# Block 2's first feed-forward with its last eight inner tiles split into latent and context, and queries ahead of keys

## The chip, the cores and the metric

The kernel is one program on one core of a Trainium2 chip. The metric is the time of one execution on the device, in microseconds (us); lower is better. Five engines work side by side, each through its own queue in order: TensorE (PE in the profile; PEld is its loading of weights), VectorE (DVE), ScalarE (ACT), GpSimd (POOL) and SyncE (SP), which here only issues transfers.

## The reference, cut to what matters

Two transformer blocks follow each other. The second has 512 latent tokens `x` and 256 context tokens `ctx`, all 1024 wide. What the change touches is the second block's first feed-forward and the projections behind it:

```
def _modnorm(x, g_pre, shift, scale):   return _rmsnorm(x, g_pre) * (1 + scale) + shift
def _residual(x, y, g_post, gate, w):   return x + w * gate * _rmsnorm(y, g_post)
def _swiglu(h, w1, w3, w2):             return (silu(h @ w1) * (h @ w3)) @ w2       # inner width 2816

x     = _residual(x,     _swiglu(_modnorm(x,     g[0], m[0],  m[1]),  w1, w3, w2), g[1], m[2],  0.5)
h_ctx = _residual(h_ctx, _swiglu(_modnorm(h_ctx, g[0], mc[0], mc[1]), w1, w3, w2), g[1], mc[2], 0.5)
# then, for latent and context tokens, from _modnorm(., g[2], m[3], m[4]) @ w_in:
#   cq (768 wide)  -> rmsnorm -> @ w_uq  -> queries of 8 heads (64 without, 32 with rotation)
#   ckv (256 wide) -> rmsnorm -> @ w_ukv -> keys and values of 8 heads;  kr (32 wide) -> rotated key part
#   qa, ka, va     -> neighbourhood attention
```

Queries are needed for the latent tokens alone, keys and values for all 768 tokens.

## The kernel before

All activations stand with features on the 128 partitions and tokens along the free axis, so a product is `weights (stationary) x tokens (moving)`. Every operand is split into a high and a low part (`whi`, `wlo` for weights; `XH`, `XL` for the latent tokens, `CH`, `CL` for the context, `hh`, `hl` for the inner layer), and each product is three matmuls: high x high, high x low, low x high.

**Weights.** `Emitter` holds a list of units. A unit is one 128x1024 block of weights (`raw`, 512 KB, three buffers), loaded by SP. It is split into two chunks of 512 columns: ACT copies the high part (`whi`, line 132), then DVE or POOL subtracts it (`wlo`, line 136; `low_parts(V, G)` says that chunks alternate between DVE and POOL, `low_parts(V, V)` that DVE makes all). Four chunk buffers run round, so the split can be at most four chunks ahead of PE. A unit over one segment of tokens is 24 matmuls (8 steps of the inner dimension x 3), recorded at line 231, into the PSUM tiles `psg` and `pss` in turn, four in all.

**Work between matmuls.** A generator handed to `background(gen, pace)` is advanced by one slot each time the matmuls put into the program add up to `pace` nanoseconds; `drain` runs it to its end. So a generator's instructions stand in each engine's queue between those of the matmuls' own helpers. A scheduler then orders each engine's queue; engines never reorder at run time.

**The feed-forward** (`ffn`, line 1123) has 22 inner tiles in groups of 6, 8 and 8. For each tile `pair` multiplies by a unit of `w1` and a unit of `w3`; the evacuations `e1`, `e3` (lines 1132 to 1141, and `hh`, `hl`) form the inner layer. Then `products` multiplies a group by eight units of `w2` and adds into `y` (line 1174). `XC` is the mode with two segments, 258 columns of context (two of them shift columns) and 512 of latent tokens; `XO` has two segments of latent tokens alone, 258 and 256 columns.

**The residual** (`update`, line 1178) works on a range of tokens of `y`: sums of squares and their reciprocal root (small DVE steps named `rsm`, a small matmul for the sums, line 330, and one that spreads the result, line 349), then for each of 8 feature tiles: `y` times the factor (line 1231, six of eight on POOL), `x` plus scaled `y` (line 1228, DVE), the new high part and the square (ACT), the low part (line 1212, DVE), the sum of squares (line 1214, seven of eight on POOL). At its end it asks for the next norm's factor `R4`, which every later evacuation multiplies by.

**The end of the feed-forward before**: the last group's eight tiles run over all 768 tokens; `products` runs over columns 256 to 767, then over 0 to 255 with `update(256, 768)` in the background; then `kv(XC_A)` (two units for `ckv`, one for `kr`, over the context and the upper latent half) with `update(0, 256)` in the background; `drain`; `kv(X_B)` (the same three units for the lower latent half, loaded again); six units of `cq`; four of `wuk` (keys), one of `wuv` (values, six chunks of tokens, spilled to memory as `v_d` through `vst`); two and four of `wuq` (queries, spilled as `qr_d`, `qn_d`). Neighbourhood attention (`open_na`) follows.

Of the kernel before, what the change touches and what calls it, by code (L numbers as in the profile page):

```python
# [6 lines left out]
F32 = mybir.dt.float32  # L7
F32R = mybir.dt.float32r
# [250 lines left out]
def emit(tc, d, out, dbg=None, stop=None):  # L259
# [756 lines left out]
                V.tensor_scalar_mul(cf(o), cf(o), w)  # L1016
        yield

    def shift_cols(kx, kc):
        todo = [(S["XH"], S["XL"], 512 + i, mod(kx)) for i in range(2)]  # L1020
        if kc is not None:
            todo += [(S["CH"], S["CL"], 0, mod(kx)), (S["CH"], S["CL"], 1, mod(kc, 1))]
        for h_, l_, o, m_ in todo:
            act(h_[:, :, o], m_)
            sub_lo(V, l_[:, :, o], m_, h_[:, :, o])
# [97 lines left out]
    def ffn(tag, w1, w3, w2, mode, ntok, pool, Rk, down, head, tail):  # L1123
# [26 lines left out]
        for gi, (k0, nk) in enumerate(grp):  # L1150
            em.call(newh)

            def pair(j, m, a=0, k0=k0):
                proj(w1[k0 + j], 128, m, e1(j), (tag, 1, a))
                proj(w3[k0 + j], 128, m, e3(j), (tag, 3, a))

            def products(segs, gi=gi, k0=k0, nk=nk):
                for n in range(8):
                    em.gemm(w2[n][:, k0:k0 + nk, :], 128, lambda si: st["h"], segs,
                            lambda si, ps, n=n: down(gi, n, segs[si][0], segs[si][1], ps), kt=nk)  # L1160

            for j in range(head(pair) if gi == 0 else 0, nk):
                pair(j, mode)
            if gi == 2:
                tail(products)
            else:
                products([(512, 256), (0, 512)] if ntok == 768 else [(0, 512)])

# [9 lines left out]
    def update(c0, c1, p, b, a, bc=None, ac=None, spilled=False, late=1500):  # L1178


        xe = min(c1, 512)
        n = xe - c0
        Ry, acc = S["Ry"][:, c0:c1], S["accy"][:, c0:c1]
        ctx = c1 > 512
        CR, SQ = {}, {}
# [5 lines left out]

        def parts(k):

            yield S["y"][:, k, c0:xe], S["x"][:, k, c0:xe], b, a, S["XH"][:, k, c0:xe], S["XL"][:, k, c0:xe], 0
            if ctx:
                yield S["y"][:, k, xe:c1], CR[k], bc, ac, S["CH"][:, k, 2:258], S["CL"][:, k, 2:258], n

        load(0)
        load(1)
# [55 lines left out]
    def no_head(pair):  # L1255
        return 0

    def f1_tail(products):
        products([(256, 512)])
        em.low_parts(V, V)  # L1260
        em.call(lambda: shift_cols(3, 3))
        em.background(lambda: update(256, 768, S["fpa"], B1X, A2X, B1C, A2C, True), 1150)
        products([(0, 256)])
        em.drain()

    em.call(open_f1)
# [5 lines left out]
    def open_pj():  # L1272
        dp = S["dram"]
        S["qn_d"] = dp.tile([4, 128, 2, 512], F32R, name="qn_d")
        S["qr_d"] = dp.tile([2, 128, 2, 512], F32R, name="qr_d")
        S["kn_d"] = dp.tile([4, 128, 2, 768], F32R, name="kn_d")
        S["kr_d"] = dp.tile([32, 2, 768], F32R, name="kr_d")
        S["v_d"] = dp.tile([8, 128, 6, 128], F32R, name="v_d")
        for n_ in ("yp", "fpa", "mp"):
            pools.close(n_)  # L1280
        p = S["pj"] = pools.open("pj", side="right")
        S["QH"] = p.tile([128, 6, 512], F32R, name="QH")
        S["QL"] = p.tile([128, 6, 512], F32R, name="QL")
        S["Rq"] = p.tile([128, 512], F32, name="Rq")
        S["aq"] = p.tile([128, 512], F32, name="aq")
        S["tmpq"] = p.tile([128, 512], F32, name="tmpq")
        for n_, w in (("rotT", 128), ("ropeC", 512), ("ropeS", 512)):
            S[n_] = p.tile([128, w], F32, name=n_)
            SP.dma_start(S[n_], d[n_])

    def open_kvp():
# [7 lines left out]
        S["tmpk"] = p.tile([128, 768], F32, name="tmpk")  # L1299
        S["krt"] = p.tile([32, 768], F32, name="krt")  # L1300
        S["krs"] = p.tile([32, 2, 768], F32R, name="krs")

    def lat_evac(j, hi, lo, acc, g, nt, last, done):
        def f(t0, n, ps, b):
# [90 lines left out]
        proj(d["wkr"], 32, mode, kr_evac, "kr")  # L1395

    em.call(open_kvp)
    em.depth(DEEP, 2)
    em.background(lambda: update(0, 256, S["fpa"], B1X, A2X, spilled=True), 1200)
    kv(XC_A)  # L1400
    em.depth(DEEP, 2)
    em.drain()
    em.call(lambda: dumps((("x2", lambda: S["x"]),)))
    em.call(open_pj)
    em.low_parts(V, G)
    kv(X_B)
    em.depth(DEEP)
    for j in range(6):
        proj(d["wq"][12 + j], 128, XO, lat_evac(j, "QH", "QL", "aq", "gq", 512, j == 5, rq_done), "cq")
    for j in range(4):  # L1410
        em.gemm(d["wuk"][j], 128, lambda si: (S["KH"], S["KL"]), [(512, 256), (0, 512)],
                nope_evac(j, "kn_d", "Rkv", 768), kt=2)
    em.gemm_tok(d["wuv"], 512, lambda si: (S["KH"], S["KL"]), [(128 * c, 128) for c in range(6)], v_evac, kt=2)
    for j in range(2):
        em.gemm(d["wuq"][4 + j], 128, lambda si: (S["QH"], S["QL"]), FULL, qr_evac(j), kt=6)
    for j in range(4):
        em.gemm(d["wuq"][j], 128, lambda si: (S["QH"], S["QL"]), FULL, nope_evac(j, "qn_d", "Rq", 512), kt=6)


    NA = {}  # L1420
# [1 line left out]
    def open_na():  # L1422
        em.flush_after()
        pools.close("pj")
        pools.close("kvp")
        p = S["onap"] = pools.open("onap", side="right")
        S["ONH"] = p.tile([128, 4, 512], F32R, name="ONH")
# [422 lines left out]
            SP.dma_start(out[:, k, c0:c1], x)  # L1850
            yield

    def f2_tail(products):
        products([(256, 256)])
        em.low_parts(V, V)
        em.background(lambda: finish(256, 512), 1100)
        products([(0, 256)])
        em.background(lambda: finish(0, 256), 1000)
        em.drain()
# [120 lines left out]
```

## Time and profile before

| what | value |
| --- | --- |
| median of 3 runs | 2838.61 us (2836.48 to 2839.34) |
| profiled execution | 2835.9 us; its trace spans 2834.1 us |
| mean granted TensorE clock | 0.984 of full speed |
| busy share of the span | PE 97%, PEld 85%, DVE 57%, ACT 39%, POOL 31% |
| weights and data moved | 316.95 MB, mean 112 GB/s |

The time between the trace's span and the profiled execution (1.8 us) lies around the program. Matmuls are pipelined and their ends are modelled: a busy PE may still be issuing slower than it could, so the distance between the starts of matmuls says more than the busy time.

### The profile page before, as it was taken

To read this page: it belongs to the slowest core of one execution; us is meant where nothing else is said; L and a number is where in the kernel's file an instruction comes from. 1 tells how busy PE (TensorE), PEld (TensorE's weight loads), DVE (VectorE), ACT (ScalarE), POOL (GpSimd) and SP (SyncE) were. 2 spreads that over 40 slices of the span, in tenths; PEclk is the share of its full clock that TensorE was granted. 3 is DMA by queue.
4 is the path that set the end of the run, shared out by engine and by line. 5 is a ranking of instruction groups with operands and counts; after the bars stand their busy time and mean duration, and the time that the engine had idled before them with its cause. 6 is when DMAs were issued, how large, how long until landed. Compare 5 with 4: busy or idle time off the path is not lost.

```text
span 2834.1 us, 42927 instructions
## 1 busy us (share of the span) xinstructions
PE 2737.6 (97%) x16308; PEld 2405.3 (85%) x16308; DVE 1619.8 (57%) x3308; ACT 1091.7 (39%) x2198; POOL 870.4 (31%) x723
## 2 busy tenths in 40 slices
PE   9999999999999889899999999979999999899997
PEld 7889988898878667788888888878889998899897
DVE  6554422377756999555223233496676876834346
ACT  4323322355534222243222122354455665633233
POOL 2213323443324233342111111442333224323224
PEclk9999999999999999999999999989999999999998
DMA  3212222443235658332121221334643425432224
GB/s 130 79 62 96 91 96 97 132 120 108 81 105 183 202 194 290 118 108 68 52 75 60 60 68 60 91 118 155 177 104 102 133 62 161 133 97 90 92 95 127
DMA packets 115998, 316.95 MB, mean 112 GB/s; under 512 B 21680, under 2 KB 35376, under 8 KB 115536
## 3 DMA queue, kind: packets, MB, share of 16 engines
q1 hardware_dynamic: 115792, 314.21, 35.8%
q8 instruction: 129, 2.11, 0.3%
q14 instruction: 77, 0.63, 0.1%
HBM read 279.09 MB, written 13.83 MB: 103 GB/s over the span
## 4 chain that ended last, share of the span: by engine, by line
PE 81%; DVE 13%; issue 3%; ACT 2%; DMA 1%; POOL 0%; SPq 0%; POOLq 0%; DVEq 0%; ACTq 0%
PE psg L231 49%; PE pss L231 23%; DVE wlo L136 2%; DVE wa L999 2%; DVE wx L999 1%; PE pss L277 1%; PE pst L831 1%; PE pss L278 1%; PE pss L279 1%; PE pst L1735 1%; PE pst L1721 1%; PE pss L1532 1%; PE pst L828 0%; DVE XL L1212 0%; DVE mg L1228 0%
## 5 line engine op out<-in xcount | busy, mean ns | idle before, releaser
L136 POOL TENSOR_TENSOR wlo<-raw,whi 128x512 fp32r<-128x512 f32 (+1 forms) x450 | 592.7, 1317 | 1571.3 <-ACT whi L132 1518.1
L132 ACT ACTIVATE whi<-raw 128x512 fp32r<-128x512 f32 (+1 forms) x844 | 522.7, 622 | 928.0 <-PE psg L231 593.1
L136 DVE TENSOR_TENSOR wlo<-raw,whi 128x512 fp32r<-128x512 f32 x394 | 306.5, 778 | 454.0 <-ACT whi L132 453.2
L231 PE MATMUL psg<-xh,wlo 128*128 128x264 f32 (+2 forms) x1104 | 361.0, 327 | 1.9 <-DVE wlo L136 1.9
L231 PE MATMUL psg<-xl,whi 128*128 128x264 f32 (+2 forms) x1104 | 362.1, 328 | 0.8 <-DVE xl L403 0.7
L231 PE MATMUL psg<-xh,whi 128*128 128x264 f32 (+2 forms) x1104 | 360.7, 327 | 0.1
L231 PE MATMUL psg<-XH,whi 128*128 128x256 f32 (+3 forms) x984 | 307.7, 313 | 2.4 <-DVE krt L1341 1.4
L231 PE MATMUL psg<-XH,wlo 128*128 128x256 f32 (+3 forms) x984 | 307.6, 313 | 0.0
L231 PE MATMUL psg<-XL,whi 128*128 128x256 f32 (+3 forms) x984 | 307.3, 312 | 0.0
L231 PEld LDWEIGHTS psg<-xh,wlo 128*128 128x128 f32 x1104 | 208.5, 189 | 18.7 <-DVE wlo L136 2.1
L231 PEld LDWEIGHTS psg<-xl,whi 128*128 128x128 f32 x1104 | 208.5, 189 | 18.6 <-DVE xl L403 1.5
L231 PEld LDWEIGHTS psg<-xh,whi 128*128 128x128 f32 x1104 | 208.6, 189 | 17.1 <-ACT whi L132 0.4
L231 PE MATMUL pss<-XL,whi 128*128 128x256 f32 (+2 forms) x600 | 190.8, 319 | 5.9 <-DVE XL L1212 5.9
L231 PEld LDWEIGHTS psg<-XH,whi 128*128 128x128 f32 (+1 forms) x984 | 185.0, 188 | 12.1 <-issue 3.1
L231 PEld LDWEIGHTS psg<-XH,wlo 128*128 128x128 f32 (+1 forms) x984 | 185.2, 188 | 10.5 <-issue 0.2
L231 PEld LDWEIGHTS psg<-XL,whi 128*128 128x128 f32 (+1 forms) x984 | 185.3, 188 | 9.3
L231 PE MATMUL pss<-XH,wlo 128*128 128x256 f32 (+2 forms) x600 | 191.1, 319 | 1.2 <-DVE wlo L136 1.2
L231 PE MATMUL pss<-XH,whi 128*128 128x256 f32 (+2 forms) x600 | 190.5, 318 | 0.5 <-DVE fs L1132 0.5
L231 PEld LDWEIGHTS pss<-XL,whi 128*128 128x128 f32 x600 | 114.3, 191 | 14.2 <-DVE XL L1212 7.2
L231 PEld LDWEIGHTS pss<-XH,wlo 128*128 128x128 f32 x600 | 114.9, 192 | 10.1 <-DVE wlo L136 1.6
L231 PEld LDWEIGHTS pss<-XH,whi 128*128 128x128 f32 x600 | 114.4, 191 | 7.5 <-DVE fs L1132 0.7
L999 DVE CUSTOM_DVE_ANT_0 wa<-wa,sb 128x1024 f32<-128x1024 f32 x72 | 106.6, 1483 | 4.4 <-DMA wa<-wa 3.9
(562 smaller groups left out, 6461.7 us busy)
## 6 DMA issues: line engine op xcount, KB each, us to landing
raw<-w SPq DMA_DIRECT2D x142, 512.0 KB, 3.4
raw<-wi SPq DMA_DIRECT2D x96, 512.0 KB, 3.3
wa<-wa SPq DMA_DIRECT2D x72, 512.0 KB, 4.2
raw<-wq SPq DMA_DIRECT2D x38, 512.0 KB, 3.5
raw<-wu SPq DMA_DIRECT2D x32, 512.0 KB, 4.1
raw<-wd SPq DMA_DIRECT2D x32, 512.0 KB, 4.2
raw<-wb SPq DMA_DIRECT2D x24, 512.0 KB, 3.3
raw<-wo SPq DMA_DIRECT2D x24, 512.0 KB, 3.6
```

What stands on the lines that cost most here:

```text
L132: s.nc.scalar.activation(h, raw, AF.Copy)
L136: eng.tensor_sub(l, raw, h.bitcast(F32))
L231: nc.tensor.matmul(out, l, r, start=(k == 0 and m == 0), stop=(k == it.kt - 1 and m == 2))
L277: T.matmul(o, wh, xh, start=first, stop=False)
L278: T.matmul(o, wh, xl, start=False, stop=False)
L279: T.matmul(o, wl, xh, start=False, stop=last)
L831: T.matmul(o, x[:, c, :], vs[:, c, :], start=False, stop=c == b and m == 1)
L999: V.tensor_tensor_reduce(o, w, sb[:, s_, :], 1.0, 0.0, ALU.mult, ALU.add, S["modc"][:, s_, j:j + 1])
L1532: T.matmul(ps[:, a:a + cw], q, k[:, c0:c0 + cw], start=m == 0, stop=m == 1)
L1721: T.transpose(ps[:, 128 * c:128 * c + 128], P_[:, 128 * (c0 + c):128 * (c0 + c) + 128], ident)
L1735: T.matmul(o[:, 0:256], v[:, c, :], x[:, c, :], start=c == 0 and m == 0, stop=c == 5 and m == 1)
```

## The change

The last group of the feed-forward is cut in two by tokens. Its eight tiles first run for the latent tokens (mode `XO`), then `products` over columns 0 to 511; then the same eight pairs of units are loaded again and run for the context (258 columns), with `update(0, 512)` in the background at one slot per 3000 ns and all low parts of weights on DVE; then `products` over the context. Behind it the six units of `cq` run, with the context's `update(512, 768)` in the background at 1700 ns; then `kv` once over all 768 tokens, the queries' units, and last the keys' and values'. The pool with the query tiles moves to another place (`pjq`).

```diff
-            for j in range(head(pair) if gi == 0 else 0, nk):
-                pair(j, mode)
+            if gi < 2 or ntok == 512:
+                for j in range(head(pair) if gi == 0 else 0, nk):
+                    pair(j, mode)
             if gi == 2:
-                tail(products)
+                tail(products, pair)
...
-            yield S["y"][:, k, c0:xe], S["x"][:, k, c0:xe], b, a, S["XH"][:, k, c0:xe], S["XL"][:, k, c0:xe], 0
+            if n:
+                yield S["y"][:, k, c0:xe], S["x"][:, k, c0:xe], b, a, S["XH"][:, k, c0:xe], S["XL"][:, k, c0:xe], 0
...
-    def f1_tail(products):
-        products([(256, 512)])
+    def f1_tail(products, pair):
+        for j in range(8):
+            pair(j, XO, "x")
+        products([(0, 512)])
         em.low_parts(V, V)
-        em.call(lambda: shift_cols(3, 3))
-        em.background(lambda: update(256, 768, S["fpa"], B1X, A2X, B1C, A2C, True), 1150)
-        products([(0, 256)])
+        em.call(lambda: shift_cols(3, None))
+        em.background(lambda: update(0, 512, S["fpa"], B1X, A2X, spilled=True), 3000)
+        for j in range(8):
+            pair(j, XC[0:1], "c")
+        products([(512, 256)])
         em.drain()
...
     em.call(open_kvp)
-    em.depth(DEEP, 2)
-    em.background(lambda: update(0, 256, S["fpa"], B1X, A2X, spilled=True), 1200)
-    kv(XC_A)
-    em.depth(DEEP, 2)
+    em.low_parts(V, G)
+    em.call(lambda: shift_cols(3, 3, False))
+    em.background(lambda: update(512, 768, S["fpa"], None, None, B1C, A2C), 1700)
+    for j in range(6):
+        proj(d["wq"][12 + j], 128, XO, lat_evac(j, "QH", "QL", "aq", "gq", 512, j == 5, rq_done), "cq")
     em.drain()
     em.call(lambda: dumps((("x2", lambda: S["x"]),)))
     em.call(open_pj)
-    em.low_parts(V, G)
-    kv(X_B)
-    em.depth(DEEP)
-    for j in range(6):
-        proj(d["wq"][12 + j], 128, XO, lat_evac(j, "QH", "QL", "aq", "gq", 512, j == 5, rq_done), "cq")
+    kv(XC)
+    for j in range(2):
+        em.gemm(d["wuq"][4 + j], 128, lambda si: (S["QH"], S["QL"]), FULL, qr_evac(j), kt=6)
+    for j in range(4):
+        em.gemm(d["wuq"][j], 128, lambda si: (S["QH"], S["QL"]), FULL, nope_evac(j, "qn_d", "Rq", 512), kt=6)
     for j in range(4):
         em.gemm(d["wuk"][j], 128, lambda si: (S["KH"], S["KL"]), [(512, 256), (0, 512)],
                 nope_evac(j, "kn_d", "Rkv", 768), kt=2)
     em.gemm_tok(d["wuv"], 512, lambda si: (S["KH"], S["KL"]), [(128 * c, 128) for c in range(6)], v_evac, kt=2)
-    for j in range(2):
-        em.gemm(d["wuq"][4 + j], 128, lambda si: (S["QH"], S["QL"]), FULL, qr_evac(j), kt=6)
-    for j in range(4):
-        em.gemm(d["wuq"][j], 128, lambda si: (S["QH"], S["QL"]), FULL, nope_evac(j, "qn_d", "Rq", 512), kt=6)
```

Three places show what stands where. On PE, behind the last matmul of the last group's products over 512 columns, this stood before:

```order
L231 MATMUL pss<-hl,whi 128x512
L231 MATMUL pss<-hh,wlo 128x512
L231 MATMUL psg<-hh,whi 128x256
L231 MATMUL psg<-hl,whi 128x256
L231 MATMUL psg<-hh,wlo 128x256
```

And this stands there now:

```order
L231 MATMUL pss<-hl,whi 128x512
L231 MATMUL pss<-hh,wlo 128x512
L231 MATMUL psg<-CH,whi 128x258
L231 MATMUL psg<-CL,whi 128x258
L231 MATMUL psg<-CH,wlo 128x258
```

Products over 256 latent columns (`hh`, `hl`) gave way to the context's pairs (`CH`, `CL`); 384 matmuls of those stand ahead of the next products.

On DVE, in the middle of the residual update (`mg` is `x`, `cr` the context's input), this stood before, among the evacuations of products:

```order
L1174 TENSOR_TENSOR y<-pss,y 128x256
L1228 SCALAR_TENSOR_TENSOR mg<-y,cf,mg 128x256
L1228 SCALAR_TENSOR_TENSOR cr<-y,cf,cr 128x256
L136 TENSOR_TENSOR wlo<-raw,whi 128x512
L1212 SCALAR_TENSOR_TENSOR XL<-mg,cf,XH 128x256
L1212 SCALAR_TENSOR_TENSOR CL<-cr,cf,CH 128x256
```

And this stands there now, among the evacuations of the context's pairs (`bt`, `fs`; lines 1228 and 1212 have become 1230 and 1214):

```order
L1230 SCALAR_TENSOR_TENSOR mg<-y,cf,mg 128x512
L136 TENSOR_TENSOR wlo<-raw,whi 128x512
L1117 COPY bt<-pss 128x2
L1132 TENSOR_TENSOR fs<-pss,R_8754 128x256
L1214 SCALAR_TENSOR_TENSOR XL<-mg,cf,XH 128x512
L1230 SCALAR_TENSOR_TENSOR mg<-y,cf,mg 128x512
L136 TENSOR_TENSOR wlo<-raw,whi 128x512 x2
```

The four steps of 256 columns for each feature tile became two of 512, and up to four low parts of weights, not one, now stand between the steps of one feature tile and the next.

On SP, where neighbourhood attention opens (`nmask`, `J` are its first loads), this stood before:

```order
L105 DMA raw<-wq 128x1024
L304 DMA qn_d<-st 256x1x512
L1431 DMA nmask<-nmask 128x896
L1433 DMA J<-J 128x128
L1444 DMA nE<-rpb 16x8x48 x8
```

And this stands there now:

```order
L105 DMA raw<-wq 128x1024
L304 DMA v_d<-vst 128x8x128 x4
L1436 DMA nmask<-nmask 128x896
L1438 DMA J<-J 128x128
L1449 DMA nE<-rpb 16x8x48 x8
```

The values' spills (`v_d`), which had the queries' units behind them, now end right ahead of the next stage's loads.

## Rows read from the trace of the kernel before

**Rows 1.** Busy time by stretch; last three columns: granted clock, DMA share, GB/s.

```profile
core 0: us, PE busy (x) PEld busy (x) DVE busy (x) ACT busy (x) POOL busy (x), PEclk, DMA share, GB/s
1643.80:1778.70 134.90, 134.90 (x769) 118.04 (x768) 49.78 (x88) 38.22 (x65) 26.65 (x24) 1.00 0.20 63
1778.70:1823.50 44.80, 44.80 (x193) 36.04 (x192) 13.32 (x18) 15.07 (x24) 17.86 (x14) 1.00 0.32 95
1823.50:1905.60 82.10, 65.05 (x439) 59.70 (x438) 72.55 (x154) 43.05 (x99) 37.37 (x33) 0.85 0.34 107
1905.60:1947.40 41.80, 39.22 (x311) 37.34 (x310) 30.57 (x85) 19.85 (x46) 14.43 (x14) 1.00 0.25 74
1836.80:1871.50 34.70, 23.20 (x134) 21.40 (x134) 34.67 (x49) 19.45 (x47) 20.00 (x16) 0.75 0.31 98
```

**Rows 2.** Chain of waits in order of time: start us, us, what.

```profile
1770.45 8.43 PE pss L231 x48
1927.43 5.75 PE pss L231 x48
```

**Rows 3.** PE's waits from 1823.5 to 1947.4: us in total, times, longest.

```profile
PE pss L231 <- DVE wlo L136: 6.0, 4, 2.4
PE psg L231 <- DVE wlo L136: 5.5, 3, 2.3
PE pss L231 <- DVE XL L1212: 3.2, 3, 1.7
```

**Rows 4.** DVE's instructions in order of time: start us, us, what.

```profile
1838.25 1.51 DVE L1228 SCALAR_TENSOR_TENSOR cr<-y,cf,cr 128x256 f32<-128x256 f32 x1
...
1841.36 0.41 DVE L1174 TENSOR_TENSOR y<-pss,y 128x256 f32<-128x256 f32 x1
1841.70 1.17 DVE L1228 SCALAR_TENSOR_TENSOR mg<-y,cf,mg 128x256 f32<-128x256 f32 x1
...
1847.15 0.47 DVE L1228 SCALAR_TENSOR_TENSOR mg<-y,cf,mg 128x256 f32<-128x256 f32 x1
1847.55 0.47 DVE L1228 SCALAR_TENSOR_TENSOR cr<-y,cf,cr 128x256 f32<-128x256 f32 x1
...
1848.34 0.68 DVE L136 TENSOR_TENSOR wlo<-raw,whi 128x512 fp32r<-128x512 f32 x1
1848.94 0.47 DVE L1212 SCALAR_TENSOR_TENSOR CL<-cr,cf,CH 128x256 fp32r<-128x256 f32 x1
```

**Rows 5.** POOL's instructions in order of time: start us, us, what.

```profile
1834.99 9.01 POOL L1231 TENSOR_TENSOR y<-y,Ry 128x512 f32<-128x512 f32 x6 [2.24 <-ACT Ry L271]
```

**Rows 6.** Groups, 1836.8 to 1871.5: count, busy us, mean ns, idle before.

```profile
L1228 DVE SCALAR_TENSOR_TENSOR mg<-y,cf,mg 128x256 f32<-128x256 f32 x8 | 9.7, 1209 | 1.2 <-POOL y L1231 1.2
L136 DVE TENSOR_TENSOR wlo<-raw,whi 128x512 fp32r<-128x512 f32 x10 | 8.4, 838 | 0.0
L1212 DVE SCALAR_TENSOR_TENSOR XL<-mg,cf,XH 128x256 fp32r<-128x256 f32 x8 | 4.8, 602 | 0.0
...
L1214 POOL TENSOR_TENSOR accy<-accy,sq 128x512 f32<-128x512 f32 x6 | 9.0, 1503 | 7.1 <-ACT sq L271 7.1
L1231 POOL TENSOR_TENSOR y<-y,Ry 128x512 f32<-128x512 f32 x5 | 7.2, 1479 | 0.0
L925 POOL TENSOR_TENSOR accy<-accy,sq 128x256 f32<-128x256 f32 x5 | 4.6, 925 | 7.6 <-ACT sq L271 4.4 <-DVE wlo L136 3.2
```

**Rows 7.** Chain of waits: small matmuls of the norms, start us, us.

```profile
1826.34 1.05 PE pst L330 x8
...
1833.18 1.10 PE pst L349 x2
...
1923.01 1.53 PE pst L349 x4
```

**Rows 8.** Busy time by stretch, in the second feed-forward; columns as in Rows 1.

```profile
2404.60:2422.60 18.00, 13.66 (x102) 12.27 (x101) 17.37 (x26) 13.25 (x32) 11.93 (x13) 1.00 0.37 117
2783.00:2806.00 23.00, 22.26 (x186) 21.99 (x185) 16.51 (x34) 11.83 (x22) 12.37 (x14) 1.00 0.56 173
```

**Rows 9.** Chain of waits: where the values' spill stands in it.

```profile
1962.11 5.49 DMA v_d<-vst
```

**Rows 10.** PE's instructions in order of time, at the lower clock.

```profile
1849.46 0.41 PE L231 MATMUL psg<-hh,whi 128*128 128x256 f32 x1
1849.67 0.41 PE L231 MATMUL psg<-hl,whi 128*128 128x256 f32 x1
```

**Rows 11.** Transfers of this weight group: KB each, median us to landing.

```profile
raw<-w SPq DMA_DIRECT2D x142, 512.0 KB, 3.4
```

More of the change, by code (lines that the diff above doesn't have):

```diff
@@ L1017, in ada_bg, with shift_cols @@
         yield
-    def shift_cols(kx, kc):
-        todo = [(S["XH"], S["XL"], 512 + i, mod(kx)) for i in range(2)]
+    def shift_cols(kx, kc, lat=True):
+        todo = [(S["XH"], S["XL"], 512 + i, mod(kx)) for i in range(2)] if lat else []
         if kc is not None:
@@ L1181, in update @@
         xe = min(c1, 512)
-        n = xe - c0
+        n = max(xe - c0, 0)
         Ry, acc = S["Ry"][:, c0:c1], S["accy"][:, c0:c1]
@@ L1192, in parts @@
         def parts(k):
-            yield S["y"][:, k, c0:xe], S["x"][:, k, c0:xe], b, a, S["XH"][:, k, c0:xe], S["XL"][:, k, c0:xe], 0
+            if n:
+                yield S["y"][:, k, c0:xe], S["x"][:, k, c0:xe], b, a, S["XH"][:, k, c0:xe], S["XL"][:, k, c0:xe], 0
             if ctx:
-                yield S["y"][:, k, xe:c1], CR[k], bc, ac, S["CH"][:, k, 2:258], S["CL"][:, k, 2:258], n
+                yield S["y"][:, k, 512:c1], CR[k], bc, ac, S["CH"][:, k, 2:258], S["CL"][:, k, 2:258], n
         load(0)
@@ L1281, in open_pj @@
         p = S["pj"] = pools.open("pj", side="right")
[L1282 to L1286, printed above, removed]
         for n_, w in (("rotT", 128), ("ropeC", 512), ("ropeS", 512)):
@@ L1301, in open_kvp @@
         S["krs"] = p.tile([32, 2, 768], F32R, name="krs")
+        p = S["pjq"] = pools.open("pjq")
+        S["QH"] = p.tile([128, 6, 512], F32R, name="QH")
+        S["QL"] = p.tile([128, 6, 512], F32R, name="QL")
+        S["Rq"] = p.tile([128, 512], F32, name="Rq")
+        S["aq"] = p.tile([128, 512], F32, name="aq")
+        S["tmpq"] = p.tile([128, 512], F32, name="tmpq")
     def lat_evac(j, hi, lo, acc, g, nt, last, done):
@@ L1424, in open_na @@
         pools.close("pj")
+        pools.close("pjq")
         pools.close("kvp")
@@ L1851, in finish, with f2_tail @@
             yield
-    def f2_tail(products):
+    def f2_tail(products, pair):
         products([(256, 256)])
```

## The prediction

> **What bounds the kernel now.** The page first: PE is busy for nearly the whole span, so a time can only fall where PE starts its matmuls late. The table by stretch then says where. The last group's pairs take 134.9 us and its products over 512 columns 44.8 us, both with PE busy throughout and the clock at 1.00. The next 82.1 us are different: PE busy 65.05, DVE 72.55, clock 0.85. The 41.8 us behind them are nearly whole again [rows 1]. The chain of waits gives the size of a unit: 48 matmuls over 258 and 256 columns start within 5.75 us, so a unit over one such segment is 2.88 us; 48 over 258 and 512 columns take 8.43 us [rows 2]. By that price the 82.1 us hold eight units of products and nine of `kv` (three units, three segments), 17 x 2.88 = 48.9 us: **33.2 us too long**. The 41.8 us hold twelve units of `cq`, 34.5 us: **7.3 us too long**. Together 40.5 us are to be had here; the chip does nothing else there that a reordering could save.
>
> The table of waits says what PE waits for: low parts of weights and the update's `XL`, both made on DVE [rows 3]. The order of time on DVE says why DVE is late. A step of 256 columns with both inputs in SBUF starts 0.40 us before the next one, a low part of 512 columns 0.60 us, an evacuation from PSUM of 256 columns 0.34 us; but the same step takes 1.51 us while POOL works [rows 4]. POOL's six multiplications of 512 columns take 9.01 us, 1.50 each [rows 5]; 1.50 less the 0.40 of a DVE step that goes in between leaves 1.10 us in which POOL holds DVE off. For 256 columns I take half, 0.55.
>
> A test of this on the worst stretch, 34.7 us long: its groups hold 32 update steps on DVE (8 `mg`, 8 `XL`, and as many for the context), 10 low parts, and on POOL 11 operations of 512 columns and 5 of 256 [rows 6]. 32 x 0.40 + 10 x 0.60 + 11 x 1.10 + 5 x 0.55 = 33.7 us, plus two more DVE steps of 512 columns (1.2): 34.9 against 34.7 measured, with DVE busy for 34.67 [rows 1]. So here DVE's steps with two SBUF inputs and POOL's steps take turns, and their **sum** is the stretch's time. The Trainium skill has a harder rule (SBUF — State Buffer, Who interferes with whom): the two engines share a port pair, which one of them holds for its whole instruction while the other is fully blocked. With POOL's whole recorded length for a hold (means of 1503, 1479 and 925 ns, [rows 6]) the stretch would come to 41 us, and the change's pairs below to 7.5 us more than I forecast, a median of 2833. The measured 34.7 refuses that length and bears out the taking of turns; I give the harder reading no chance of its own.
>
> **The change part by part.** *Streaming.* Removed: 16 units of 8.43 = 134.9. Added: 16 of 5.75 (`XO`) and 16 of 2.88 (context) = 138.1, +3.2 us. `kv` goes from nine segments, 25.9 us, to three units of 8.43, 25.3: -0.6. Products keep their 67.8 us in another order, `cq` its 34.5. Sum: **+2.6 us**. The `XO` pairs are the form that the second feed-forward runs at 5.75 us; I charge no stall there, and none for their products, which ran whole at 44.8.
>
> *The context's pairs with `update(0, 512)`.* At 3000 ns a slot, 4 slots go to the norm and 11 carry the work, 33 us of matmuls: some 12 of the 16 units, 34.5 us of PE. What takes turns in them: 24 low parts (14.4); 6 steps `fs` of 256 columns (2.4); 16 update steps of 512 columns at 0.66 (10.6; no row in the open has them, so 0.40 plus the 0.26 by which a 512-column low part exceeds a 256-column evacuation; bounds 0.60 and 0.80); three more DVE steps (1.8); on POOL 13 operations of 512 columns (14.3) and 6 of 256 for `hl` (3.3). Sum **46.8 us against 34.5**: 12.3 too long. From above: if DVE's 12 evacuations and bias copies find no POOL time to hide under, +5, 17. From below: the four chunk buffers (1.44 us of PE each) let DVE fall 5.8 us behind before PE notices, and the products behind the pairs are light enough to catch up: 6.5, and 5.5 with the cheaper step. Between the ends I take **10**, nearer the full sum, as the worst stretch kept it. The 32 added low parts are in this; so is the POOL work, which the change neither adds nor removes.
>
> *`cq` with the context's update.* DVE: 16 update steps, 12 `QL` (all 0.40), three more (1.0), six low parts (3.6) = 15.8. POOL: six low parts (6.6), 21 steps of 256 columns (11.6) = 18.2. Sum 34.0 against 34.5 of PE, with rsqrt and PSUM evacuations under POOL's time. Full, but not over: **3**, bounds 0 and 12 (all of DVE's 16 us of other steps in series, less what four PSUM tiles buffer).
>
> *Norms.* The small matmuls on the chain, six pieces from 1826.34 to 1923.01 of up to 1.5 us [rows 7], some 6 us in all, remain; with a wait or two **7**.
>
> *The tail.* Keys and values now stand ahead of neighbourhood attention. The values' spill holds the chain for 5.49 us before the queries [rows 9]; that wait moves to the attention's start, and behind it SP has the attention's first loads, whose tiles lie where `vst` lay. Bounds 0 and 8; **3**.
>
> *Clock.* The clock fell to 0.75 where PE was busy 23.2 of 34.7 us [rows 1], but stood at 1.00 in a stretch of the second feed-forward with 13.66 of 18.0 busy [rows 8], a share close to what I expect in the context's pairs (34.5 of 45). **2**, bounds 0 and 35 (below).
>
> *Transfers.* 16 more units of 512 KB and 2 MB of spilled `x` make 10.5 MB in some 56 us, 187 GB/s. Products in the second feed-forward drew 173 GB/s with PE busy 22.26 of 23.0 us [rows 8], and a unit lands in 3.4 us with three in flight [rows 11]. Nothing, if it stays so; SP's spills wait for DVE steps that the next `raw` waits for anyway.
>
> Sum: too long after the change 10 + 3 + 7 + 3 + 2 = 25, and 2.6 of streaming; 40.5 - 27.6 = **12.9 us saved**. The profiled execution (2835.9) becomes 2823.0; it lies 2.7 under the median, so the median becomes **2825.7**.
>
> **The rivals.** *The cover is whole.* The update hides altogether; the pairs lose 2, `cq` 1, norms 6, the tail 0: 9 + 2.6, saved 28.9, 2809.7. For it: slots 2.6 times as far apart as now. Against it: 46.8 against 34.5.
>
> *`cq` and the tail eat it.* `cq` loses 12 and the tail 8, as their upper bounds say: 10 + 12 + 7 + 8 + 2 + 2.6 = 41.6, 1 us slower, 2839.7, which measures as no change. For it: DVE and POOL are as full in `cq` as PE. Against it: nothing needs the context's update until `kv`, so PE can run ahead by four PSUM tiles.
>
> *The lower clock, and slower.* At the lower clock matmuls of 256 columns start 0.21 us apart [rows 10], a unit is 5.04 us. If short waits for low parts keep the clock there through all 16 context units, these take 80.6 us in place of 46.0: 34.6 + 3 + 7 + 3 + 2.6 = 50.2, **9.7 us slower**, 2848.3. It decides from about twelve units on: 12 x 2.16 = 26, twice what the pairs and the clock are charged above. For it: the 0.75. Against it: rows 8.
>
> *Transfers bind.* If 173 GB/s were the limit, 10.5 MB would take 61 us, 5 more than the 56 forecast: saved 8, 2830.7.
>
> **How the numbers follow.** Forecast 0.55, whole cover 0.12, `cq` and tail 0.15, lower clock 0.10, transfers 0.08. The likeliest gives 2825.7; its own range, from the terms' nearer bounds (pairs 5.5 to 17, tail 0 to 5), is 2816 to 2834. 8 in 10 reach from 2811, most of the whole cover, to 2842, past the no-change rival and short of the clock's. This kernel's runs scatter by about 0.1%, so 0.2%, 5.7 us, is what can be told from no change: faster are forecast, whole cover and transfers, less 0.05 at the forecast's end: 0.70; same 0.05 + 0.15 = 0.20; slower 0.10.
>
> **What would show it.** `XO` pairs at 5.75 us with no wait; context units 2.9 us at first, then 3.5 to 4.2, waiting for `wlo` on DVE, whose steps there swell beside POOL's; `cq` near 6 us a unit; a stop of some us around `v_d` at the attention's start. I would be wrong if DVE had gaps in the context's pairs (cover whole), if the clock's row showed under 0.8 there, or if PE waited at `cq` for DVE's evacuations more than 5 us in all.

## The result and the profile after

The changed kernel is slower: median 2859.23 us (2856.69 to 2864.42, 4 runs) against 2838.98 us (2836.48 to 2840.54, 4 runs) of the kernel before, ratio 1.0075 with a 95% interval of 1.0063 to 1.0086. That is 20 us the wrong way; the forecast was 2825.7, the range ended at 2842. The profiled executions say the same, 2854.9 us of span against 2834.1. From here on a ratio is always that to the kernel before on the same chip, and 0.01% is 0.28 us. The first lines of the page:

```profile
span 2854.9 us, 43697 instructions
## 1 busy us (share of the span) xinstructions
PE 2740.1 (96%) x16620; PEld 2418.9 (85%) x16620; DVE 1617.0 (57%) x3351; ACT 1106.0 (39%) x2221; POOL 882.6 (31%) x730
```

The table by stretch, with columns as in [rows 1], answers to that group: `XO` pairs, their products, context pairs, their products, `cq`, `kv`, keys and values, start of the attention. (The queries, 1952.20 to 1980.30, are left out.)

```profile
1646.71:1738.78 92.07, 92.07 (x770) 92.06 (x768) 40.69 (x88) 33.88 (x65) 27.63 (x24) 1.00 0.29 92
1738.78:1783.58 44.80, 44.80 (x195) 36.04 (x193) 12.46 (x19) 14.97 (x24) 18.06 (x14) 1.00 0.30 94
1783.58:1841.40 57.82, 51.91 (x396) 50.18 (x395) 53.19 (x97) 34.32 (x64) 24.59 (x19) 0.94 0.51 165
1841.40:1870.90 29.50, 25.79 (x205) 24.53 (x204) 21.12 (x49) 15.60 (x33) 6.95 (x8) 1.00 0.53 162
1870.90:1911.50 40.60, 37.39 (x301) 36.10 (x300) 34.68 (x76) 21.31 (x50) 23.67 (x24) 1.00 0.23 74
1911.50:1952.20 40.70, 35.19 (x174) 27.05 (x173) 22.31 (x76) 12.75 (x28) 4.91 (x5) 0.87 0.17 54
1980.30:2007.00 26.70, 17.07 (x86) 14.01 (x84) 15.78 (x27) 11.80 (x21) 4.82 (x6) 0.87 0.98 332
2007.00:2017.00 10.00, 10.00 (x71) 10.00 (x72) 2.38 (x6) 2.79 (x5) 3.95 (x4) 0.84 0.67 180
```

Where the 20.8 us of the traces lie:

| part | before | after | |
| --- | --- | --- | --- |
| up to the first matmul of the last group | 1643.77 | 1646.71 | +2.9 |
| from there to the attention's first matmul | 353.56 | 360.24 | +6.7 (forecast -12.9) |
| attention's start to its output projection | 216.21 | 227.42 | +11.2 |
| from there to the end | | | 0.0: -2.7 in the output projection, +3.3 in the stage whose input is `M2H` (the last projection ahead of the second feed-forward), rest -0.6 |

The first part's queues are the same in both kernels but for four steps of 8 columns, two on ACT and two on DVE, which stand behind it now. Over the runs below the same matmul starts anywhere from 1643.9 to 1649.0, so 2.9 is how executions differ, not the change.

PE's waits in the new `kv` and at the attention's start; the first answers to [rows 3], the last to [rows 9]:

```profile
PE pst L349 <- DVE RF L340: 4.7, 1, 4.7
PE pst L330 <- DVE akv L925: 0.8, 1, 0.8
...
PE psg L231 <- DVE vst L1396: 9.6, 1, 9.6
```

The first of them in PE's order of time, twelve matmuls into `kv` (it answers to [rows 7]):

```profile
1912.69 0.28 PE L231 MATMUL psg<-CL,whi 128*128 128x258 f32 x1
1912.81 0.28 PE L231 MATMUL psg<-CH,wlo 128*128 128x258 f32 x1
1917.82 0.90 PE L349 MATMUL pst<-RF,ones 128*128 128x256 f32 x2 [4.73 <-DVE RF L340]
1918.16 0.78 PE L231 MATMUL psg<-CH,whi 128*128 128x258 f32 x1
```

None of the `kv` products needs `RF`; the small matmul that spreads the context's norm merely stands ahead of them in PE's queue. Behind the wait the clock is lower: 0.87 for the stretch, so a part of it ran at the lower of the clock's two levels. The chain of waits through the values' end:

```profile
1994.14 6.24 DMA v_d<-vst
...
2000.47 0.70 ACT vst L271
2001.16 0.02 issue
2001.19 0.76 DVE vst L1396
2001.95 0.02 issue
2001.97 3.29 DMA v_d<-vst
```

Spill, copy, spill: a new `vst` can't be written until one of its two buffers has been spilled, and PE's next product waits for the PSUM tile that the copy reads. Before, such a spill held the chain for 5.49 us [rows 9]; now PE waits 9.6, and the attention opens at a granted clock of 0.84.

### The profile page after: what moved, and what is told of

The parts are those of the page before. It is cut to its first block, busy times and chain, and to the rows that moved or that the text cites. A ratio compares the mean times of both kernels' runs of the same rounds, so it can differ in the third digit from the quotient of the medians.

```text
span 2854.9 us, 43697 instructions
## 1 busy us (share of the span) xinstructions
PE 2740.1 (96%) x16620; PEld 2418.9 (85%) x16620; DVE 1617.0 (57%) x3351; ACT 1106.0 (39%) x2221; POOL 882.6 (31%) x730
## 4 chain that ended last, share of the span: by engine, by line
PE 77%; DVE 15%; issue 3%; DMA 2%; ACT 2%; POOL 0%; SPq 0%; POOLq 0%; DVEq 0%; ACTq 0%
PE psg L231 47%; PE pss L231 21%; DVE wlo L136 2%; DVE wa L999 2%; DVE wx L999 1%; PE pss L277 1%; DMA wa<-wa 1%; PE pst L831 1%; PE pss L278 1%; PE pst L1740 1%; PE pss L279 1%; PE pst L1726 1%; PE pss L1537 1%; ACT whi L132 1%; PE pst L828 0%
## 5 line engine op out<-in xcount | busy, mean ns | idle before, releaser
L132 ACT ACTIVATE whi<-raw 128x512 fp32r<-128x512 f32 (+1 forms) x871 | 539.6, 622 | 898.4 <-PE psg L231 560.6
L136 DVE TENSOR_TENSOR wlo<-raw,whi 128x512 fp32r<-128x512 f32 (+1 forms) x422 | 321.4, 762 | 377.8 <-ACT whi L132 374.7
L231 PE MATMUL psg<-XH,whi 128*128 128x256 f32 (+2 forms) x1040 | 319.3, 307 | 11.1 <-DVE vst L1396 9.6
L231 PE MATMUL psg<-XL,whi 128*128 128x256 f32 (+2 forms) x1040 | 319.9, 308 | 3.3 <-DVE XL L1214 3.3
L231 PE MATMUL psg<-XH,wlo 128*128 128x256 f32 (+2 forms) x1040 | 320.5, 308 | 0.9 <-DVE wlo L136 0.6
L231 PEld LDWEIGHTS psg<-XH,whi 128*128 128x128 f32 x1040 | 197.3, 190 | 20.6 <-issue 12.6
L231 PEld LDWEIGHTS psg<-XL,whi 128*128 128x128 f32 x1040 | 197.6, 190 | 12.1 <-DVE XL L1214 3.9
L231 PEld LDWEIGHTS psg<-XH,wlo 128*128 128x128 f32 x1040 | 197.9, 190 | 11.0 <-DVE wlo L136 1.0
L231 PEld LDWEIGHTS pss<-XH,whi 128*128 128x128 f32 x648 | 122.0, 188 | 5.9 <-ACT whi L132 1.2
L231 PEld LDWEIGHTS pss<-XL,whi 128*128 128x128 f32 x648 | 122.3, 189 | 4.8
```

Source lines behind the costliest of these rows:

```text
L132: s.nc.scalar.activation(h, raw, AF.Copy)
L136: eng.tensor_sub(l, raw, h.bitcast(F32))
L231: nc.tensor.matmul(out, l, r, start=(k == 0 and m == 0), stop=(k == it.kt - 1 and m == 2))
```

## The experiments

Each edit is to the changed kernel unless it says otherwise, and was timed beside the kernel before.

**The order of the last units** (e1, e2). e1 puts keys and values ahead of the queries again; e2 takes the kernel before and makes the projections' order that of the change.

```diff
-    kv(XC); wuq (rotated 2, others 4); wuk 4; wuv
+    kv(XC); wuk 4; wuv; wuq (rotated 2, others 4)          # e1, on the changed kernel
-    kv(X_B); cq 6; wuk 4; wuv; wuq
+    cq 6; kv(X_B); wuq; wuk 4; wuv                         # e2, on the kernel before
```

> The changed kernel, with the order of the last units put back: keys and values ahead of the queries. Theory A (the tail and what hangs on it cost some 14 us): the 9.6-us wait for vst at the end falls under 1 us at the attention's start, the first attention unit is back at 2.9 us, and attention's matmuls, which the scheduler then puts in the order that they had before the change, win back some 6 us; the key units, now right behind the kv units, pay some 3 us for the wait on Rkv. 2859.2 - 14 + 3 = about 2848. Theory B (the time behind the changed stretch went by drift from execution to execution, not by the order): 2856 to 2862.

> The kernel before, with only its projections in the order of the change: cq ahead of the second half of kv, then queries, keys, values. Its feed-forward and its updates stay, and attention's matmuls stand as before. Theory A1 (spills of keys and values back to back are what is late): the values' units and the attention's start lose some 6 + 2, so 2839.0 + 8 = about 2847, with a wait for vst of more than 5 us at the end. Theory A2 (attention itself starves because the spilled keys and values land late): also the 6 us inside attention, about 2853. Theory B (the order is not what cost it): 2837 to 2841.

e1: 2845.22 us, 1.0031 (1.0020 to 1.0042), so 0.44%, 12.5 us, of the 0.75% come back. e2: 2844.84, 1.0027 (1.0016 to 1.0038), 8 us slower than before. Theory A holds and B falls. In e2 the attention takes 221.60 us, but all 5.4 us above 216.21 lie in its first two units (6.64 and 4.43 us in place of 2.90 and 2.86); behind them every unit keeps its distance. So A2 falls as well: the attention doesn't starve, only its start is late.

**Mixed order, and more buffers** (e8, e12).

```diff
+    for f in (qr[0], qr[1], uk[0], uk[1], qn[0], uk[2], uk[3], qn[1]) + tuple(uv) + (qn[2], qn[3]): f()   # e8
-        o = p.tile([128, 8, 2, 64], F32R, name="vst", tag="vst", bufs=2)
+        o = p.tile([128, 8, 2, 64], F32R, name="vst", tag="vst", bufs=6)                                  # e12
```

> The changed kernel, with the last units mixed: both rotated query units, two of keys, one of queries, two of keys, one of queries, the values, two of queries. Theory A1 (DMA is the limit where 6.2 MB of keys and values are spilled in some 27 us at 332 GB/s): spreading them over the queries' 28 us takes the wait for vst away wholly, 13 to 16 us less than the changed kernel, and 1 to 3 us less than e1, where the values still took 15.5 us. Rival: as e1 or worse, because the wait for vst is a matter of the values' own six spills through two buffers and not of what is spilled around them.

> The changed kernel, with six buffers for vst in place of two, so that no values' unit waits for a spill. Theory A1 (the queue of spills is bound by what the transfers move, 332 GB/s): the 9.6-us wait of PE at vst goes, but the attention's start, whose loads stand behind the spills on SP, takes most of it: within 3 us of the changed kernel's 2859. Rival (the two buffers are the limit): 6 to 9 us less.

e8: 2844.23, 1.0026 (1.0016 to 1.0037), no different from e1, so it doesn't tell A1 from its rival. (That median is over all eight executions; without the profiled one, which took 9657 us, it is 2843.75. No trace of e8 is used.) e12: 2845.36, 1.0029 (1.0018 to 1.0040): 13 us won by four more buffers, where theory A1 wanted the spills' bandwidth to keep it within 3, and the rival 6 to 9. By stretch, keys and values and then the attention's start, in e12, and PE's wait at their end:

```profile
1978.78:1996.00 17.22, 17.05 (x86) 13.97 (x84) 14.21 (x26) 11.38 (x21) 3.06 (x3) 1.00 0.96 341
1996.00:2005.00 9.00, 9.00 (x74) 8.96 (x75) 3.41 (x8) 2.90 (x6) 4.62 (x7) 1.00 1.09 327
...
PE psg L231 <- DVE vst L1396: 0.2, 1, 0.2
```

17.2 us in place of 26.7, at the same transfer rate (341 against 332 GB/s), and the attention's first unit is at 3.00 us (2.90 before, 4.44 after). The transfers were full all the while; PE waited only for a buffer. A1 falls: the two buffers are the cause of the wait.

**The context's update and the norms in `cq` and `kv`** (e3, e7, e11, e13). Edits in one:

```diff
-    em.background(lambda: update(512, 768, S["fpa"], None, None, B1C, A2C), 1700)
+    ... 1400)                          # e3
+    ... gap=6200), 1600)               # e7 and e13: the spread's matmul later behind the sums' (was 3200)
+    ... G=V), 1700)                    # e11: the update's POOL steps on DVE
-    em.drain(); open_pj; kv(XC)
+    em.depth(DEEP, 2); kv(XC)          # e7, e13: drain (e7) and open_pj inside kv, behind its first unit
-        em.after(2500, f)              # queries' and keys' norms, with gap=2800
+        em.after(5000, f)              # e13, with gap=7000; nothing is drained ahead of kv
```

> The changed kernel, with the context's update behind cq at one slot per 1400 ns in place of 1700, so that its norm's sums stand 94 matmuls earlier on PE (in the fifth of six cq units, not in the sixth). Theory C (the kv units were late because PE's queue held the spread of that norm 12 matmuls into them, and the clock then fell): the wait of 4.7 us and the lower clock behind it go, 8 to 10 us: about 2850. Rival D (DVE and POOL are as full as PE in cq, so an earlier sum waits there as long): 2857 to 2861. Rival E (only the wait goes, the clock stays low): about 2854.5.

> The changed kernel, with the context update at 1600 ns a slot, its norm's spread 57 matmuls behind its sums (in the run e3 it was 40, in the changed kernel 26), and the evacuations of the first kv unit put behind both its segments, so that none waits for the spread. Theory C' (the sum can't be made before some 32.3 us into cq, when DVE and POOL have done the update, and the chain to the spread takes some 6 us: PE waits wherever sums and spread stand earlier than that): sums and spread now stand just there, no wait for accy or RF over 1 us, cq about 38, kv about 32: 9 to 10 us less than the changed kernel's 40.6 + 40.7. Rival D (full engines push the wait on): less than 4 us.

> The changed kernel, with only the context's update behind cq on DVE (13 steps of 256 columns); update(0, 512) stays. Theory L (what stops PE at the start of kv is that DVE is behind by the time cq ends: in e3 and e7 the wait only moved from one norm's matmul to the other's): DVE's backlog shrinks by 13 x 0.15 to 13 x 0.3 = 2 to 4 us, and cq and kv together, 81.3 us, by as much. Theory C (the place of the spread in PE's queue alone): no change, 80 to 82.

> The changed kernel with all three norms between cq and the queries loosened on PE, nothing else: the context's sums at 1600 ns a slot and its spread 57 matmuls behind; the sums of the queries' and keys' norms 5000 ns behind their last evacuation in place of 2500, their spreads 7000 in place of 2800; the pool is reopened behind the first kv unit, so that nothing is flushed ahead of kv, whose first evacuations come behind both its segments. Theory M (each norm is a chain of some 6 us through DVE, and PE stopped because all its matmuls stood within 26 matmuls of each other: move one and the next one stops it): no wait for accy, RF, aq, tmpq or akv over 1 us, cq 37 to 39, kv 27 to 30, together 13 us less than the changed kernel's 81.3: about 1.003. Theory L (DVE is behind by what it has to do, wherever the norms stand): less than 4 us.

| run | median | ratio (interval) | `cq` | `kv` | both |
| --- | --- | --- | --- | --- | --- |
| changed | 2859.23 | 1.0075 (1.0063 to 1.0086) | 40.6 | 40.7 | 81.3 |
| e3 | 2854.07 | 1.0058 (1.0045 to 1.0071) | 46.5 | 31.9 | 78.4 |
| e7 | 2855.05 | 1.0067 (1.0055 to 1.0080) | 40.0 | 41.1 | 81.1 |
| e11 | 2853.78 | 1.0056 (1.0043 to 1.0068) | 44.2 | 33.9 | 78.1 |
| e13 | 2852.69 | 1.0048 (1.0035 to 1.0061) | 40.0 | 32.4 | 72.4 |

PE's waits over `cq` and `kv` in e3, then in e7, then in e13:

```profile
PE pst L349 <- ACT RF L271: 3.8, 2, 3.1
PE pst L330 <- DVE accy L1216: 2.9, 1, 2.9
```

```profile
PE pst L330 <- DVE aq L925: 3.6, 1, 3.6
PE pst L349 <- DVE RF L340: 1.9, 1, 1.9
```

```profile
PE pst L349 <- DVE RF L340: 1.9, 1, 1.9
```

In e3 `kv` won 8.8 us as theory C said, with its clock back at 1.00, and `cq` lost 5.9: the sums now wait for the update itself (`accy`), and their spread for `RF`. (The total is the one that rival E named, but E's reason, a clock that stays low, doesn't hold.) In e7 the spread of the context's norm waits 1.9 us in place of 4.7, and the queries' sums (`aq`), next in PE's queue, wait 3.6. So C alone falls, and C' too; the wait moves from one norm to the next. Loosening all three wins 8.9 us of `cq` and `kv`, between what theories M (13) and L (under 4) asked, and leaves 1.9 at one norm: these 8.9 were chains of DVE steps of some 6 us with too little PE work between their ends, and the lower clock behind the waits (`kv` at 0.95 in place of 0.87). e11's 3.2 us are what L expected of it, so DVE's load has a part too. With both, in e14 below, `kv` takes 28.7 us, PE busy throughout and the clock at 1.00; `cq` takes 43.7. What of e13's 72.4 us against 59.8 of streaming is left was not taken apart further.

**POOL's steps given to DVE** (e5, e10), and a slower pace (e6).

```diff
-        em.background(lambda: update(0, 512, S["fpa"], B1X, A2X, spilled=True), 3000)
+        ... spilled=True, G=V), 3000)      # e5: in update, G is then DVE
+        ... spilled=True), 3400)           # e6
-    update(256, 768, ...), 1150); update(0, 256, ...), 1200)
+    update(256, 768, ..., G=V), 1150); update(0, 256, ..., G=V), 1200)     # e10, on the kernel before
```

> The changed kernel, with the thirteen steps of update(0, 512) that POOL makes (six products of y with Ry, seven sums of squares) given to DVE; nothing leaves the computation. Theory H (steps of DVE with two SBUF inputs and steps of POOL take turns, so only their sum counts, and POOL holds DVE off for 1.10 us where DVE itself needs 0.66): 13 x 0.44 = 5.7 us less in the context's pairs, 57.8 to about 52, and the kernel some 5 us under the changed kernel. Rival I (the two engines work side by side and DVE is the one that is full): DVE gets 13 x 0.66 = 8.6 us more to do, the pairs go to some 66 us, the kernel 8 over the changed kernel.

> The changed kernel, with update(0, 512) at one slot per 3400 ns in place of 3000, so that more of it lies beside the products over the context. Pairs and products took 57.8 + 29.5 = 87.3 us for 69 of streaming. Theory J (the pairs are late because DVE and POOL together are over-full there, and the products have room): pairs about 53, products 30 to 31, together 3 to 4 us less. Rival K (the products are as full: their 16 low parts and 8 evacuations and the norm): what the pairs win the products lose, together 86 to 88.

> The kernel before, with the POOL steps of both its updates (13 of 512 columns, 13 of 256) on DVE. Theory H (POOL's steps and DVE's take turns, POOL's hold is longer than DVE's own step): at 1.10 us a hold 13 x 0.44 + 13 x 0.15 = 7.7 us off the 82.1-us stretch, at the 1.39 us that e5 gives back per step more: 2826 to 2832. Rival I (DVE is what is full; it gets some 14 us more): 2842 or more. It also says whether the change itself, or only its updates' place on the engines, is worth something.

e5: 2847.21, 1.0034 (1.0021 to 1.0048). The pairs of the context in e5:

```profile
1785.84:1834.11 48.27, 47.95 (x395) 47.26 (x394) 44.76 (x99) 33.05 (x61) 7.13 (x7) 1.00 0.57 188
```

Groups of DVE and POOL in that stretch, of the changed kernel first, then of e5:

```profile
L136 DVE TENSOR_TENSOR wlo<-raw,whi 128x512 fp32r<-128x512 f32 x29 | 23.6, 818 | 1.7 <-ACT whi L132 1.5
L1230 DVE SCALAR_TENSOR_TENSOR mg<-y,cf,mg 128x512 f32<-128x512 f32 x8 | 10.1, 1260 | 1.2 <-POOL y L1233 1.2
...
L1233 POOL TENSOR_TENSOR y<-y,Ry 128x512 f32<-128x512 f32 x6 | 9.7, 1653 | 0.0
L1216 POOL TENSOR_TENSOR accy<-accy,sq 128x512 f32<-128x512 f32 x6 | 8.8, 1474 | 9.6 <-ACT sq L271 9.6
```

```profile
L136 DVE TENSOR_TENSOR wlo<-raw,whi 128x512 fp32r<-128x512 f32 x28 | 19.3, 688 | 1.7 <-ACT whi L132 1.5
L1230 DVE SCALAR_TENSOR_TENSOR mg<-y,cf,mg 128x512 f32<-128x512 f32 x7 | 5.7, 809 | 0.0
L1233 DVE TENSOR_TENSOR y<-y,Ry 128x512 f32<-128x512 f32 x7 | 4.8, 703 | 0.4 <-ACT Ry L271 0.4
```

In the pairs the same low part takes 688 ns instead of 818, the same `mg` step 809 instead of 1260, and the pairs fell by 9.5 us, to 2.3 above streaming. DVE was busy there for 44.76 us in place of 53.19, but some of its work moved into the products behind, which took 30.3 us in place of 29.5. Over both stretches DVE was given more steps and was busy for less: 157 instructions in 71.18 us in place of 145 in 74.31. Theory H holds, and rival I, an independent DVE that is simply full, falls.

Both stretches together fell by 8.75 us, to 78.57. Per step moved that is 8.75 / 13 = 0.67 us, which with DVE's own 0.66 makes a hold of 1.33, not 1.10; but the granted clock of the pairs, 1.00 in place of 0.94, has up to 3.5 us of it (0.06 of 57.8), and without these the hold is 1.06. The changed kernel's own trace gives it more directly. Two DVE steps of 512 columns that each stand beside a step of POOL:

```profile
1806.49 1.75 DVE L1214 SCALAR_TENSOR_TENSOR XL<-mg,cf,XH 128x512 fp32r<-128x512 f32 x1
1808.17 1.75 DVE L136 TENSOR_TENSOR wlo<-raw,whi 128x512 fp32r<-128x512 f32 x1
1809.84 0.15 DVE L1117 COPY bt<-psg 128x2 f32<-128x2 f32 x1
```

They start 1.68 and 1.67 us ahead of what follows, where a low part alone takes 0.60 [rows 4]: POOL holds DVE off for some 1.08 us, near the 1.10. A sum of 512 columns on POOL with no DVE step beside it, in the products over the latent columns:

```profile
1757.57 1.29 POOL L925 TENSOR_TENSOR accy<-accy,sq 128x512 f32<-128x512 f32 x1
```

So POOL's recorded 1.47 to 1.65 us beside DVE have some waiting of its own in them. e10: 2831.79, 0.9974 (0.9965 to 0.9983): the 82.1-us stretch of [rows 1] took 75.0, 7.1 less where holds of 1.10 and 0.55 gave 7.7 (its clock rose as well, from 0.85 to 0.89). So a plain edit to the kernel before wins 7 us without the reordering. e6: 2859.19, 1.0076 (1.0064 to 1.0089); pairs and products 58.84 + 29.58 = 88.4: nothing won, rival K.

**The queues behind the gates** (e4).

```diff
-    em.low_parts(V, G)                                            # ahead of open_m2, and at the end of f2_head
+    em.low_parts(G, V)
+    em.call(lambda: setattr(em, "rot_i", em.rot_i + 3))           # ahead of open_m2
```

> The changed kernel, with the weights' chunks behind the gate stage given to DVE and POOL the other way round and the PSUM tiles' turn moved on by three, so that every engine's queue from that stage to the end is that of the kernel before. Theory F (the change made the count of chunks differ by an odd number, 27, which swapped the engines of the low parts; this is the 3.3 us lost in that stage): about 2856. Rival G (the stage is late for what comes ahead of it): 2858.5 to 2860.

2854.92, 1.0063 (1.0050 to 1.0075). The interval overlaps that of the changed kernel, and in the trace the stage of `M2H` took 56.06 us against 56.90 after and 53.63 before, with the longest wait for `M2H` at 1.6 us in place of 2.7. By itself that is inconclusive. The other traces say more, when they are set side by side at the stage's granted clock: at 1.00 the stage takes 53.6 to 54.1 us in the order of before (before, e9, e14, e16) and 55.4 in the changed kernel's (e5, e12); at 0.97 it takes 56.06 (e4) and 56.90 (after); at 0.94 the changed order takes 57.9 (e1, e3). So the swapped chunks cost 1 to 2 us, and the rest of the 3.3 goes with the clock, which was 1.00 in the trace before and 0.97 in the one after.

**Together** (e9, e14, e15, e16). e9: both updates on DVE, 1500 ns for the context's, the tail of e8, the queues of e4. e14: both updates on DVE, norms as in e13, the queues of e4, one rotated query unit, then keys, values and the other queries, three buffers for `vst`. e16: as e14 with six. e15: the kernel before with e10's edit and six buffers.

> The changed kernel with what the runs so far suggest: both updates wholly on DVE, the context's at 1500 ns, the mixed tail of e8, and the queues behind the gate stage as before (e4). If the gains add (e5 0.41%, e8 0.49%, e4 0.12% of the changed kernel's 0.75%, and 3 to 6 us in cq and kv): 0.3 to 0.5% under the kernel before. If they overlap (one wait taking the place of another, as in e3): within 0.1% of it.

> All together on the changed kernel: both updates on DVE, loose norms as in e13, one rotated query unit, then keys, values and the other queries, three buffers for vst; attention's matmuls then stand as before the change. From e9 (0.9969) less what its kv and values still lost (some 8 us in cq and kv if theory M holds, 5 at the values): 0.992 to 0.995. If theory L holds: 0.995 to 0.997.

> The kernel before, with its updates on DVE (e10, 0.9974) and six buffers for vst: the control for e14. The wait of 5.5 us at the values goes: about 0.9955. If it stays within 0.2% of e14, the reordering itself is worth nothing.

> As e14, with six buffers for vst in place of three. This alone makes the scheduler put attention's matmuls in the order that they have in the changed kernel. Theory N (that order costs some 9 us in the attention and gives 2.7 back behind it): 6 to 7 us more than e14, 0.22%, and 225 in place of 216 us from the attention's start to its output projection. Rival (the attention was late for the spills ahead of it): 0 to 2 us less than e14.

| run | median (range) | ratio (interval) |
| --- | --- | --- |
| e9 | 2828.70 (2826.53 to 2833.58) | 0.9969 (0.9959 to 0.9979) |
| e14 | 2826.42 (2820.62 to 2826.71) | 0.9951 (0.9939 to 0.9964) |
| e15, control | 2829.87 (2824.27 to 2830.90) | 0.9968 (0.9956 to 0.9980) |
| e16 | 2822.27 (2819.94 to 2823.86) | 0.9944 (0.9932 to 0.9957) |

e9 came out at the low end of what adding the gains gave, e14 just short of its own and in the range that theory L gave, with 3.4 us of wait for `accy` still in `cq`. By the mark set ahead of e15, within 0.2% of e14, the reordering would be worth nothing: 0.9968 against 0.9951. e16 beats both kernels: 16 us under the one before, 37 under the changed one. Its range and the control's don't overlap, 7.6 us between the medians: with the repairs the reordering seems worth something, at the edge of what the intervals (0.9957 and 0.9956) can tell. But e16 has loosened norms and the control doesn't; what those would win in the kernel before was not tried, so the gain isn't shown to be the reordering's.

Theory N fell as it was put: e16 came out 4 us under e14, not 6 to 7 over (their intervals overlap), and its attention took 219.52 us, not 225, which is 1.0 us over the kernel before when the output projection is counted in. Its matmul order was neither that of before nor that of the changed kernel. What the traces do show is where the changed kernel's attention lost its time; four waits in PE's order of time, 38 to 40 us apart:

```profile
2033.43 0.88 PE L1557 MATMUL pst<-ident,nvt 128*128 128x128 f32 x6 [0.71 <-DVE nvt L1473]
...
2071.38 0.84 PE L1557 MATMUL pst<-ident,nvt 128*128 128x128 f32 x6 [0.80 <-DVE nvt L1473]
...
2110.97 0.85 PE L1557 MATMUL pst<-ident,nvt 128*128 128x128 f32 x6 [0.78 <-DVE nvt L1473]
...
2150.39 0.84 PE L1557 MATMUL pst<-ident,nvt 128*128 128x128 f32 x6 [0.80 <-DVE nvt L1473]
```

They come once for each of the attention's four rounds, the last 140 us after the spills, so it isn't the spills that bring them. e12, which has no wait at the values, has the same four (2.9 us in all) and 225.54 us, in a third order. e16 has none of them; PE's waits over its whole attention:

```profile
PE pst L1580 <- DVE npcl L274: 0.6, 2, 0.4
PE pst L1560 <- DVE nsm L1552: 0.3, 2, 0.2
PE pst L1577 <- DVE npxl L274: 0.2, 1, 0.2
```

Over all the traces the attention's time goes with its order: 216.0 to 216.2 us in that of the kernel before (also e1, e9, e10, e14 and e15; e2 adds its late start), 227.3 to 228.5 in that of the changed kernel (also e3 to e7, e11 and e13, all with a late start), 225.5 and 219.5 in the orders of e12 and e16. In all these orders but the first, 21 matmuls more stand ahead of the output projection, which is then 2.3 to 2.7 us shorter. So the traces put some 7 us (11.2, less 1.6 in the first units and 2.7 given back in the output projection) on the order that the scheduler gave attention's background work, which the edit never touches. No run changed that order alone, and why it turns on the tail and on the number of buffers stays open.

## Why the prediction was wrong

**What held.** The `XO` pairs (92.07 us against 16 x 5.75) and their products (44.8) are as forecast, and so is the sum of the context's pairs: 46.0 + 10 + 2 for the clock is 58.0, measured 57.82, waiting for `wlo` on DVE. That it meets to 0.2 us is in part luck. The 10 was picked between 5.5 and 17, PE waited 5.9 us in all, and it was busy for 51.91 us, 5.9 over the streaming, where 2 were charged. `cq` came to 40.6, 37.5 and its share of the norms. Transfers bound nothing in the pairs and the products, at 165 and 162 GB/s.

**The norms' 7 us and kv at no charge: the main failed step.** Products, `cq` and `kv` were to take 23.0 + 34.5 + 3 + 25.3 + 7 = 92.8 us and took 110.8. I counted what PE spends on small matmuls in [rows 7], not what stands between them: sums, a root of a dozen small DVE steps, a spread. Three such chains now end in 25 us of `kv`'s matmuls, where before the keys' norm had `cq` to hide under and the queries' norm the keys. `kv` as three units of 8.43 us named no cover because it assumed no chain. Over streaming, `kv` took 15.4 us, the products 6.5 and `cq` 6.1, of which 3 were charged to it: 25 us where 7 were to cover it all. Of `kv`'s 15.4, 5.5 were waits (`RF` and `akv`), some 5.3 the lower clock (0.13 of 40.7), and the rest, some 4.6, its 28 small matmuls. The clock's 2 us had been charged to the pairs alone. e13 gives 8.9 of `cq` and `kv` back. In the products PE waited 2.1 us for `hh` and 1.2 at the spread.

**The tail, 3 of 0 to 8: mis-sized, and with the wrong cause.** Queries, keys and values took 54.8 us against 49.9, and the first attention units 1.6 more; e2 puts the whole at 8, the upper bound. The prediction moved the spill's wait to the attention's start without a cause for it, and theory A1 then took it for one of transfers. It was a ring of two buffers (e12). [rows 9] showed that a spill stood on the chain; whether for its rate or its buffers, no row told.

**Downstream unchanged: not considered at all.** 11.2 us in the attention, -2.7 and +3.3 behind it (of the 3.3, 1 to 2 by e4 and the traces beside it). I assumed that instructions which the edit does not touch would stay where they are. In the changed kernel's queues they don't: the attention's matmuls, and behind them the PSUM tiles and the engines of the low parts, stand otherwise as far as the second feed-forward.

**The rivals.** None named the chains of the norms or the attention's order. "`cq` and the tail eat it" had the tail right at 8 and put 12 into `cq` which went to `kv`; alone it ends at no change. The lower clock, the only slower rival, didn't happen where it was looked for, 0.94 in the pairs; 0.87 came in `kv`.

**The sum of holds.** POOL's hold of 1.10 us is borne out: some 1.08 in the changed kernel's trace, 7.1 of 7.7 us in e10, and 1.33 in e5 or 1.06 without the clock's part. The Trainium skill has the rule (SBUF — State Buffer, Who interferes with whom) that one engine holds the shared ports for its whole instruction while the other is blocked. Both runs bear out its direction, but not that length: the hold was shorter than POOL's recorded 1.47 to 1.65, and than the 1.29 that its step takes alone. The prediction refused the rule with recorded lengths that hold POOL's own waiting, so it made the rule look further off than it is.

## What to carry to other kernels

Price a norm by its chain (sums, root, spread) and ask which PE work lies between its two ends; moving a stage away can leave three chains with no cover. Before calling a wait one of bandwidth, count the buffers that the waiting write goes round. Where a scheduler orders the queues, compare the order to the end of the program, not to the end of the edit.

## What was unexpected of the hardware

Transfers at 341 GB/s with their engines 96% busy cost PE nothing: 17.05 us busy of 17.22 beside them in e12. And giving an engine more steps made it less busy: DVE in the context's pairs and the products behind them, 74.31 to 71.18 us, once POOL's steps of the update had become its own.
